# RWKV chunk recurrence: one run of state products and one run of value products in place of alternating ones

## The chip, the cores and the metric

The kernel runs on one core of a Trainium2 chip. Its time is the device time of one execution in microseconds (us), from the first to the last instruction of the core. Besides the timed runs there is one execution recorded by the hardware profiler; all rows below are of that execution. The engines are named as in the profile: PE is the tensor engine's matmuls, PEld its weight loads, DVE the vector engine, ACT the scalar engine, POOL the GpSimd engine, SP the engine that issues most DMAs.

## The reference

The kernel computes one transformer layer on 512 tokens of 1024 features in fp32: a norm, an input projection, two mixers side by side (sparse attention with three branches on one half of the features, an RWKV-7 recurrence with 8 heads of 64 on the other), an output projection, a second norm and a squared-ReLU feed-forward of width 4096. The change lies in the recurrence, which the reference states token by token:

```python
def step(state, inp):
    r_t, w_t, k_t, v_t, a_t, b_t = inp
    sa = jnp.einsum('bhvk,bhk->bhv', state, a_t)
    state = state * w_t[:, :, None, :] + sa[..., None] * b_t[:, :, None, :] + v_t[..., None] * k_t[:, :, None, :]
    return state, jnp.einsum('bhvk,bhk->bhv', state, r_t)
```

## The kernel before

**The recurrence by chunks.** The 512 tokens are 4 tiles of 128 (index `i`), and each tile is two chunks of 64 (index `c`); `q` counts the 8 chunks. Within a chunk all tokens are worked on at once, and only the state of 8 heads (64 by 64 each) goes from chunk to chunk. Heads lie in pairs: `e` is the half of the 128 partitions, rows 0 to 63 or 64 to 127, and `f` (0 to 3) counts the pairs. Each function of a tile's work is a Python generator, a *stream*: `rw_prep(i)` makes the decayed queries and keys (`AR`, `BK`) and the products `GA` and `YL`; `rw_inv(i)` inverts the triangular matrices (`QU`); `rw_vals(i)` makes the values (`UV`) and `LV`; `rw_chain(q)` is the serial step, and `rw_out(i)` norms its result.

**One step of the chain** (line 723) has three groups of products on PE, all through one PSUM bank (`pq_`, one buffer). `pp` (line 736) multiplies the state with the keys, 8 products; DVE adds it to `LV`. `puu` (line 743) multiplies by the inverse, 8 products; ACT and DVE copy it to `UV` (lines 744 and 745). `py` has two halves: `py[:, 1]` is the chunk's output, the state times the queries (line 752, left out at `q` = 0) plus the values' product (line 754); `py[:, 0]` is what is added to the state (line 755). Lines 760 and 761 on DVE make the new state `Sn`, and line 763 on ACT copies the output to `YY`. For each of the 8 pairs `(f, e)` line 752 is issued, then 754, then 755, and then the next pair. A product of line 752 has 64 rows and 64 columns of the array (64*64 in a profile row), one of lines 754 and 755 has 128 rows and 64 columns (128*64). Each fp32 product stands in the trace as two PE instructions, so `py` is 48 instructions in a chunk, or 32 at `q` = 0.

**What sets the order.** `merge` (line 129) runs the streams by a clock of its own: a stream yields the tensor-engine time that it assumes and a delay, or a condition on other streams, and the stream of the highest priority that is due goes on. On top of this the tile framework, which schedules by a simulated timeline, places each instruction in its engine's queue; each queue is then worked off in order. So between the chain's products stand products of the attention (`sc` line 1072, `pT` line 1108, `pv` lines 1121 to 1125), of the inverse (line 681) and of the input projection (`pa`, lines 332 to 334). After the chain of the last tile, `wo_load` (line 1146) loads and splits the output weights through two `wr` buffers into places that the chain's `ar`, `uv` and `yl` tiles leave, and `outproj` (line 1177) uses them. The feed-forward comes last, from line 1264 on.

Of the kernel before, what the change touches and what calls it, by code (L numbers as in the profile page):

```python
# [16 lines left out]
# T tokens in NT tiles, D features in KD tiles; the rest orders the streams of work and their loads  # L17
T = 512
# [40 lines left out]
# places in SBUF: size of each in bytes, and how many  # L59
# [8 lines left out]
# columns of the constant array  # L68
# [46 lines left out]
def layer(ctx: ExitStack, tc: tile.TileContext, A, cst, out):  # L115
# [7 lines left out]
    # ------------------------------------------------------------- scheduling  # L123
    # Work is written as streams: a stream yields (time on the tensor engine, delay until what it
    # waits for is there), or a condition on the other streams, and the streams are merged by that.
# [30 lines left out]
    # ------------------------------------------------------------------ pools  # L156
# [24 lines left out]
    def cycle(*places):  # L181
        """Allocation that goes round some places."""
        k = [0]

        def f(shape, name, dt=F32):
            k[0] += 1
            return at(places[(k[0] - 1) % len(places)], shape, name, dt)
        return f
# [4 lines left out]
    # -------------------------------------------------------------- constants  # L193
# [15 lines left out]
    def gain_load(src, place):  # L209
        """Gains per feature, in all partitions."""  # L210
        g_ = [at(place[b], [128, 512], "gain") for b in range(2)]
        for b in range(2):
            nc.sync.dma_start(g_[b], src[0:1, b * 512:(b + 1) * 512].partition_broadcast(128))
        return g_
# [33 lines left out]
    # vectors that are used per feature, 128 features to a row  # L248
# [49 lines left out]
    # ---------------------------------------------------------------- helpers  # L298
    def rsqrt(v, n, key, p=128):
        """1/sqrt of a small array of positive numbers."""  # L300
        y = small(n, "rs_y" + key)[0:p]
        G.tensor_tensor(y, v, bc(MH[0:p], [p, n]), op=ALU.pow)
        return y
# [3 lines left out]
    def split(raw, shape, hi=None, lo=None, eng=V):  # L307
        """A matrix in two parts, which add up to it exactly."""
        hi = (hi or w_hi)(shape, "whi", F32R)
        lo = (lo or w_lo)(shape, "wlo", F32R)  # L310
        S.copy(hi, raw)  # L311
        eng.tensor_tensor(lo, raw, hi.bitcast(F32), op=ALU.subtract)  # L312
        return hi, lo
# [22 lines left out]
    def norm_T(i, x_, gain, NH_, NL_, place, pool, raw=None):  # L336
        """Token tile i, normed, into the features' layout, in two parts."""
        ss = small(2, "ss")
        tmp = [at(place, [128, 512], "nt") for _ in range(2)]
        for b in range(2):  # L340
            S.activation(tmp[b], x_[b], AF.Square, scale=1.0 / 32, accum_out=ss[:, b:b + 1])
        vv = small(1, "vv")
        V.scalar_tensor_tensor(vv, ss[:, 0:1], 1e-6, ss[:, 1:2], op0=ALU.add, op1=ALU.add)
        rs = rsqrt(vv, 1, 'n')
        for b in range(2):
            V.scalar_tensor_tensor(tmp[b], x_[b], rs, gain[b], op0=ALU.mult, op1=ALU.mult)
            pt = pool([128, 4, 128], "pt")
            for kk in range(4):
                PE.transpose(pt[:, kk, :], tmp[b][:, kk * 128:(kk + 1) * 128], ident)
            S.copy(NH_[b][:, i], pt)  # L350
            if raw:
                S.copy(raw[b], pt)
            V.tensor_tensor(NL_[b][:, i], pt, NH_[b][:, i].bitcast(F32), op=ALU.subtract)

    # ------------------------------------------------------------ input norm
# [5 lines left out]
    def xk(k, i0=0, i1=NT):  # L361
        """The rows of a group of features, for tokens tiles i0 to i1."""
        return XH[k // 4][:, i0:i1, k % 4, :], XL[k // 4][:, i0:i1, k % 4, :]
# [6 lines left out]
    # =============================================================== RWKV  # L370
# [30 lines left out]
    # blocks of projected columns in the order of their use  # L401
# [6 lines left out]
    def turn_of(n):  # L408
        """A part of the input products waits for the one before it."""
        k = ORD.index(n)  # L410
        return lambda: ('in', ORD[k - 1]) in done if k else 'rw_kr' in done
# [8 lines left out]
    def raw_piece(p_):  # L420
        """A piece before it is split."""
# [6 lines left out]
    def piece(c0, h):  # L428
        """The next piece of the input weights; those after it are on their way."""
# [13 lines left out]
    def feat_cols(c0, use, halves=False):  # L443
        """Two tiles of 128 projected columns, features in the partitions."""
# [83 lines left out]
    def rw_prep(i):  # L528
# [49 lines left out]
        # products of keys with queries  # L578
# [26 lines left out]
    def rw_vals(i):  # L605
# [3 lines left out]
        # values, tokens in the partitions: odd heads in rows 0-63, even ones in rows 64-127  # L609
# [9 lines left out]
        # the bonus takes the place of the values in their other layout  # L619
# [25 lines left out]
    def rw_inv(i):  # L645
# [3 lines left out]
        # inverse of the triangular matrices: blocks of 32, merged from 2 up  # L649
# [73 lines left out]
    def rw_chain(q):  # L723
# [22 lines left out]
        yield 0.7, 0.8  # L746
        py = pq_([128, 2, 4, 64], "py")
        for f in range(4):
            for e in range(2):
                uv = UV[e][:, 4 * c + f, :]  # L750
                if q:
                    PE.matmul(py[ROW[1 - e], 1, f, :], AR[c][ROW[e], f, 1, :], S_[ROW[e], f, :],  # L752
                              start=True, stop=False)
                PE.matmul(py[ROW[1 - e], 1, f, :], YL[e][c][:, f, 1 - e, :], uv, start=not q, stop=True)  # L754
                PE.matmul(py[ROW[e], 0, f, :], YL[e][c][:, f, e, :], uv, start=True, stop=True)
# [8 lines left out]
        yield 1.8, 1.5  # L764
# [47 lines left out]
    # =============================================================== NSA  # L812
# [11 lines left out]
    def nsa_consts():  # L824
        # gains of the keys, with those of the queries and the scale
# [7 lines left out]
    def tok_cols(c0, n, use):  # L833
        """Projected columns, tokens in the partitions."""
# [12 lines left out]
    def compress(kind, ckv):  # L847
        """Compressed keys (0) or values (1)."""
# [66 lines left out]
    def keys(b, kb):  # L915
        """Keys of branch b: normed, in two parts, transposed."""
# [55 lines left out]
    def nsa_in():  # L972
# [4 lines left out]
        def cmp_in(j, pa):  # L977
            """Each token's features with those of the next one below them."""
# [11 lines left out]
        def kv_parts(b, i, pa, o0):  # L990
            """Columns o0 on of those of keys and values."""
# [49 lines left out]
    def attn_scores(i, g):  # L1041
# [5 lines left out]
        # compressed branch  # L1047
# [14 lines left out]
        # scores of the two other branches  # L1062
# [75 lines left out]
    # =============================================================== output  # L1138
# [53 lines left out]
    def norms():  # L1192
# [6 lines left out]
        for i in range(NT):  # L1199
# [6 lines left out]
            # differences of the normed tokens for the products by blocks  # L1206
# [20 lines left out]
    def run_more():  # L1227
        # the streams that others start
# [34 lines left out]
    # =============================================================== feed-forward  # L1263
# [12 lines left out]
    def blocks(b):  # L1276
        """The parts of a pair of tiles of features that its products by blocks take, in the order of their use."""
# [18 lines left out]
    def ahead_of(gens, n):  # L1296
        """What the generators give, made n parts ahead."""
# [46 lines left out]
    def pair_blocks(b):  # L1344
        """Products by blocks of two (Winograd's form of Strassen's): 7 for the 8."""
# [84 lines left out]
```

## Time and profile before

| | us |
|---|---|
| timed runs, median of 3 (lowest, highest) | 816.68 (814.18, 823.08) |
| profiled execution, first to last instruction | 818.9 |
| its PE busy time | 797.5 (97%) |
| its DVE, ACT, POOL busy time | 511.0, 395.9, 174.1 |
| from the start of the chain's first `py` (187.7) to the end of its last (410.5) | 222.8 |
| feed-forward and what follows the output projection's weights, from 440 on | 379 |

A busy PE in these rows is not a PE at its peak, since matmuls are pipelined and their ends are modelled; the distance from one instruction's start to the next one's start is what an instruction takes of the engine. The granted clock of PE stands in the rows as a share: 1.0 is 2.4 GHz and 0.5 is 1.2 GHz.

### The profile page before, as it was taken

Reading aid. Unit: us, or ns where it says so; the run is one execution under the profiler, and the core shown is the slowest. Engines: PE = TensorE matmul, PEld = TensorE weight load, DVE = VectorE, ACT = ScalarE, POOL = GpSimd, SP = SyncE. Lnnn points to the kernel's source line nnn. Section 1 sums busy time; section 2 is a strip of 40 time slices with the busy share of each in tenths; the row PEclk is TensorE's granted clock in tenths of the full one; section 3 lists DMA queues with packets and bytes.
Section 4 is the critical chain, followed back from the end, with each engine's and each line's share of the span. In section 5 each row is a group of like instructions: output and inputs, shape, how many; then the busy total and the mean of one; then the engine's idle time right before and its main releaser. Section 6 shows DMA issues by size and latency. Waiting matters only on the chain.

```text
span 818.9 us, 18281 instructions
## 1 busy us (share of the span) xinstructions
PE 797.5 (97%) x7357; PEld 684.4 (84%) x7357; DVE 511.0 (62%) x1157; ACT 395.9 (48%) x928; POOL 174.1 (21%) x176
## 2 busy tenths in 40 slices
PE   7999999999989999999999999999999999999998
PEld 5888888988878787887777889998888999978886
DVE  6344385674575399488764699986333799963333
ACT  6343334345353476569643564675332366663320
POOL 4002042312241252344320024310001323100000
PEclk9999999999975799599999999999999999999999
DMA  6741321120000000020134223314332343133212
GB/s 225 207 116 52 79 80 56 29 54 14 3 15 1 28 3 2 1 68 15 40 103 117 90 77 108 102 51 142 99 98 88 114 117 104 59 111 114 90 52 103
DMA packets 67338, 62.00 MB, mean 76 GB/s; under 512 B 6013, under 2 KB 53299, under 8 KB 67254
## 3 DMA queue, kind: packets, MB, share of 16 engines
q1 hardware_dynamic: 67254, 60.83, 24.9%
q8 instruction: 58, 0.95, 0.5%
q14 instruction: 26, 0.21, 0.1%
HBM read 58.72 MB, written 2.10 MB: 74 GB/s over the span
## 4 chain that ended last, share of the span: by engine, by line
PE 79%; DVE 11%; ACT 4%; DMA 3%; issue 2%; SPq 1%; POOL 0%; DVEq 0%; ACTq 0%; POOLq 0%
PE pa L332 7%; PE pa L333 7%; PE pa L334 7%; PE po L332 7%; PE po L333 7%; PE po L334 7%; PE pw L333 4%; PE pw L334 4%; PE pw L332 3%; PE sc L1072 3%; PE pg L586 2%; DVE wlo L312 2%; PE py L754 2%; PE py L752 2%; DMA wraw<-in_w_out_dram 2%
## 5 line engine op out<-in xcount | busy, mean ns | idle before, releaser
L311 ACT CAST whi<-wraw 128x512 fp32r<-128x512 f32 (+1 forms) x128 | 78.7, 622 | 141.5 <-PE po L333 29.1
L312 DVE TENSOR_TENSOR wlo<-wraw,whi 128x512 fp32r<-128x512 f32 (+1 forms) x120 | 86.2, 721 | 93.6 <-ACT whi L311 87.8
L332 PE MATMUL po<-whi 128*128 128x512 f32 x256 | 100.6, 394 | 1.6 <-DVE cc L1358 1.6
L333 PE MATMUL po<-wlo,whi 128*128 128x512 f32 x256 | 101.0, 395 | 0.0
L334 PE MATMUL po<-whi,wlo 128*128 128x512 f32 x256 | 100.7, 393 | 0.0
L333 PE MATMUL pw<-TT,whi 128*128 128x256 f32 x224 | 63.2, 282 | 0.0
L334 PE MATMUL pw<-TT,wlo 128*128 128x256 f32 x224 | 63.0, 281 | 0.0
L332 PE MATMUL pw<-TT,whi 128*128 128x256 f32 x224 | 62.5, 279 | 0.0
L332 PEld LDWEIGHTS po<-whi 128*128 128x128 f32 x256 | 48.0, 188 | 13.5 <-ACT whi L311 2.0
L334 PEld LDWEIGHTS po<-whi,wlo 128*128 128x128 f32 x256 | 48.1, 188 | 11.4
L333 PEld LDWEIGHTS po<-wlo,whi 128*128 128x128 f32 x256 | 48.1, 188 | 11.0
L332 PE MATMUL pa<-XH,whi 128*128 128x512 f32 (+1 forms) x144 | 53.6, 377 | 1.0 <-ACT XH L350 1.0
L333 PE MATMUL pa<-XL,whi 128*128 128x512 f32 (+1 forms) x144 | 54.4, 379 | 0.0
L334 PE MATMUL pa<-XH,wlo 128*128 128x512 f32 (+1 forms) x144 | 53.5, 374 | 0.0
L1086 POOL TENSOR_SCALAR P<-P,z 128x128 f32<-128x128 f32 (+3 forms) x32 | 35.6, 1122 | 77.9 <-DVE z L1035 35.5
L1288 POOL TENSOR_TENSOR ws<-wq 128x512 f32<-128x512 f32 x14 | 21.5, 1533 | 138.4 <-DMA wq<-in_w_ff_dram 123.4
L312 DVE TENSOR_TENSOR wlo<-ws,whi 128x512 fp32r<-128x512 f32 x56 | 48.1, 870 | 3.1 <-ACT whi L311 3.0
L311 ACT CAST whi<-ws 128x512 fp32r<-128x512 f32 x56 | 33.0, 618 | 34.8 <-PE pw L334 10.0
L312 DVE TENSOR_TENSOR wlo<-H,whi 128x512 fp32r<-128x512 f32 x32 | 22.1, 689 | 42.3 <-PE po L333 32.7
L334 PE MATMUL pw<-NH,wlo 128*128 128x256 f32 x168 | 47.0, 280 | 0.0
L333 PE MATMUL pw<-NL,whi 128*128 128x256 f32 x168 | 46.8, 279 | 0.0
L332 PE MATMUL pw<-NH,whi 128*128 128x256 f32 x168 | 46.8, 279 | 0.0
(319 smaller groups left out, 2109.8 us busy)
## 6 DMA issues: line engine op xcount, KB each, us to landing
wraw<-in_w_ff_dram SPq DMA_DIRECT2D x72, 256.0 KB
wq<-in_w_ff_dram SPq DMA_DIRECT2D x56, 256.0 KB
wraw<-in_w_in_dram SPq DMA_DIRECT2D x40, 256.0 KB
wraw<-in_w_in_dram SPq DMA_DIRECT2D x8, 268.0 KB
x<-in_x_dram SPq DMA_DIRECT2D x8, 256.0 KB
y<-in_x_dram SPq DMA_DIRECT2D x8, 256.0 KB
wraw<-in_w_out_dram SPq DMA_DIRECT2D x8, 256.0 KB
wraw<-in_w_out_dram SPq DMA_DIRECT2D x16, 128.0 KB
```

The source lines that it names most:

```text
L311: S.copy(hi, raw)
L312: eng.tensor_tensor(lo, raw, hi.bitcast(F32), op=ALU.subtract)
L332: PE.matmul(o_, l[0], r[0], start=first, stop=False)
L333: PE.matmul(o_, l[0], r[1], start=False, stop=False)
L334: PE.matmul(o_, l[1], r[0], start=False, stop=last)
L586: PE.matmul(pg[:, f], BK[ROW[e], 2 * f + c].rearrange("p a b -> p (a b)"), AR[c][ROW[e], f].rearrange("p a b -> p (a b)"), start=True, sto ...
L752: PE.matmul(py[ROW[1 - e], 1, f, :], AR[c][ROW[e], f, 1, :], S_[ROW[e], f, :], start=True, stop=False)
L754: PE.matmul(py[ROW[1 - e], 1, f, :], YL[e][c][:, f, 1 - e, :], uv, start=not q, stop=True)
L1072: PE.matmul(sc[:, h - h0, :], Qt[:, h, :], KT[br, g, hl].rearrange("p i t -> p (i t)")[:, 0:w], start=hl == 0, stop=hl == 1)
L1086: (G if (h, br) in SCG else V).tensor_scalar(P_[:, h, 0:w], P_[:, h, 0:w], z[:, h:h + 1], None, op0=ALU.mult)
L1288: G.tensor_tensor(s3, q[0][0], q[1][0], op=ALU.subtract)
```

## The change

In a chunk, all 8 products of the state with the queries (line 752) are issued first, and then the 16 products of the values (now line 757), in the same order of pairs. Only the first product in each half of the partitions opens the bank (`start`), where before every product with the queries and every one of line 755 did. The time that the stream tells `merge` for the group goes from 1.8 to 1.6. Comments are taken out elsewhere, and the lines after 755 move by 3.

```diff
         py = pq_([128, 2, 4, 64], "py")
-        for f in range(4):
-            for e in range(2):
-                uv = UV[e][:, 4 * c + f, :]
-                if q:
-                    PE.matmul(py[ROW[1 - e], 1, f, :], AR[c][ROW[e], f, 1, :], S_[ROW[e], f, :],
-                              start=True, stop=False)
-                PE.matmul(py[ROW[1 - e], 1, f, :], YL[e][c][:, f, 1 - e, :], uv, start=not q, stop=True)
-                PE.matmul(py[ROW[e], 0, f, :], YL[e][c][:, f, e, :], uv, start=True, stop=True)
+        FE = [(f, e) for f in range(4) for e in range(2)]
+        if q:
+            for f, e in FE:
+                PE.matmul(py[ROW[1 - e], 1, f, :], AR[c][ROW[e], f, 1, :], S_[ROW[e], f, :],
+                          start=f == 0, stop=False, skip_group_check=True)
+        for f, e in FE:
+            uv = UV[e][:, 4 * c + f, :]
+            for a, r in ((1 - e, 1), (e, 0)):
+                PE.matmul(py[ROW[a], r, f, :], YL[e][c][:, f, a, :], uv,
+                          start=not q and f == 0 and e == 0, stop=True, skip_group_check=True)
...
-        yield 1.8, 1.5
+        yield 1.6, 1.5
```

The last step (`q` = 7) shows the plain case. On PE its `py` stood so before (the first two pairs and the last):

```order
L1108 MATMUL pT<-identr,P 128x128 x8
L752 MATMUL py<-Sn,AR 64x64
L754 MATMUL py<-UV_2928,YL_2774 64x64
L755 MATMUL py<-UV_2928,YL_2774 64x64
L752 MATMUL py<-Sn,AR 64x64
L754 MATMUL py<-UV_2929,YL_2776 64x64
L755 MATMUL py<-UV_2929,YL_2776 64x64
...
L752 MATMUL py<-Sn,AR 64x64
L754 MATMUL py<-UV_2929,YL_2776 64x64
L755 MATMUL py<-UV_2929,YL_2776 64x64
L1121 MATMUL pv<-th,VH 128x512
```

and stands so now (`pv` at line 1124 is the one at 1121 before):

```order
L1111 MATMUL pT<-identr,P 128x128 x8
L752 MATMUL py<-Sn,AR 64x64 x8
L757 MATMUL py<-UV_2928,YL_2774 64x64 x2
L757 MATMUL py<-UV_2929,YL_2776 64x64 x2
...
L757 MATMUL py<-UV_2929,YL_2776 64x64 x2
L1124 MATMUL pv<-th,VH 128x512
```

The 24 products stand between the same neighbours; the 8 of line 752 are now together ahead of the 16. In the step `q` = 3 other work stands inside the group, and the scheduler moved it. A piece of the difference on PE there (`pd` and `pz` are of the inverse, `pbn` of the values of the next tile):

```order
-L752 MATMUL py<-Sn,AR 64x64
-L754 MATMUL py<-UV_1831,YL_1599 64x64
-L681 MATMUL pz<-Tn,qm 32x32 x29
+L757 MATMUL py<-UV_1831,YL_1599 64x64
+L757 MATMUL py<-UV_1830,YL_1597 64x64 x2
+L757 MATMUL py<-UV_1831,YL_1599 64x64 x2
+L681 MATMUL pz<-Tn,qm 32x32 x30
 L534 MATMUL pu<-W2A,THA 128x512
-L681 MATMUL pz<-Tn,qm 32x32 x3
-L755 MATMUL py<-UV_1831,YL_1599 64x64
```

Here the last products of `py` now come ahead of `pz` and `pu` (of the next tile's preparation), where one of them came behind both.

On SP, the piece of the queue that reloads `x` for the output projection (`y`) and loads the output weights, as a difference:

```order
-L1181 DMA y_5749<-in_x_dram 128x512
-L1156 DMA wraw<-in_w_out_dram 128x512 x4
-L1181 DMA y_5777<-in_x_dram 128x512
-L1161 DMA wraw<-in_w_out_dram 64x512 x4
+L1184 DMA y_5749<-in_x_dram 128x512
+L1159 DMA wraw<-in_w_out_dram 128x512 x4
+L1164 DMA wraw<-in_w_out_dram 64x512 x2
+L1184 DMA y_5777<-in_x_dram 128x512
+L1164 DMA wraw<-in_w_out_dram 64x512 x2
```

Two half-size loads of the output weights now stand ahead of the second reload, where all four stood behind it. The other moves on PE, DVE and ACT are of single instructions past a few neighbours in the attention from `q` = 3 on.

## Rows read from the trace of the kernel before

**Rows 1.** The page: busy time by engine, and the granted clock in 40 slices.

```profile
PE 797.5 (97%) x7357; PEld 684.4 (84%) x7357; DVE 511.0 (62%) x1157; ACT 395.9 (48%) x928; POOL 174.1 (21%) x176
PEclk9999999999975799599999999999999999999999
```

**Rows 2.** Busy time by stretch: PE, PEld, DVE, ACT, POOL, granted clock, DMA share, GB/s.

```profile
200.00:233.40 33.40, 30.86 (x699) 26.54 (x698) 20.41 (x41) 13.38 (x31) 12.30 (x12) 1.00 0.01 3
233.40:274.40 41.00, 40.24 (x284) 34.98 (x284) 21.77 (x99) 18.15 (x70) 8.83 (x9) 0.50 0.02 7
274.40:329.00 54.60, 53.30 (x966) 41.75 (x962) 45.31 (x147) 36.27 (x104) 19.92 (x19) 1.00 0.04 12
329.00:346.10 17.10, 17.10 (x116) 14.51 (x116) 7.14 (x43) 8.51 (x35) 6.02 (x8) 0.50 0.00 1
440.00:819.00 379.00, 371.17 (x2241) 328.04 (x2239) 238.55 (x396) 169.51 (x324) 50.01 (x36) 1.00 0.31 95
```

**Rows 3.** Timeline of PE, py at q = 1: start, length, instruction.

```profile
200.62 0.33 PE L752 MATMUL py<-Sn,AR 64*64 64x64 f32 x2
200.88 0.27 PE L754 MATMUL py<-UV,YL 128*64 128x64 f32 x1
...
201.14 0.33 PE L752 MATMUL py<-Sn,AR 64*64 64x64 f32 x2
...
204.78 0.75 PE L681 MATMUL pd<-Z,Q 32*32 32x32 f32 x64
```

**Rows 4.** Timeline of PE, py at q = 2, first row and the row behind.

```profile
251.73 0.47 PE L752 MATMUL py<-Sn,AR 64*64 64x64 f32 x2
...
258.23 2.08 PE L1072 MATMUL sc<-KT,QT 128*128 128x256 f32 x8
```

**Rows 5.** Timeline of PE, py at q = 0, first row and the row behind.

```profile
187.72 0.27 PE L754 MATMUL py<-UV,YL 128*64 128x64 f32 x1
...
188.80 1.16 PE L586 MATMUL pg<-AR,BK 64*128 64x128 f32 x8
```

**Rows 6.** Chain of waits, pp at full and at half clock: start, us.

```profile
192.52 0.61 PE pp L736 x16
265.18 1.05 PE pp L736 x16
```

**Rows 7.** Instructions of py alone, by stretch (q = 3 to 7): columns as in rows 2.

```profile
279.10:287.00 7.90, 4.59 (x48) 3.33 (x48) 0.00 (x0) 0.00 (x0) 1.00 0.10 33
326.10:332.50 6.40, 5.39 (x48) 3.85 (x48) 0.00 (x0) 0.00 (x0) 0.73 0.00 0
351.40:355.60 4.20, 4.20 (x48) 3.08 (x48) 0.00 (x0) 0.00 (x0) 1.00 0.00 2
394.30:398.50 4.20, 4.19 (x48) 3.08 (x48) 0.00 (x0) 0.00 (x0) 1.00 0.01 2
406.30:410.50 4.20, 4.18 (x48) 3.09 (x48) 0.00 (x0) 0.00 (x0) 1.00 0.31 106
```

**Rows 8.** Who PE waited for, 180 to 480 us: total, times, longest.

```profile
PE pz L702 <- DVE Tn L694: 3.6, 2, 3.1
```

**Rows 9.** Chain of waits, where it runs through DVE after q = 1 and q = 3.

```profile
223.85 0.35 DVE kkn L561
...
234.16 1.07 PE pz L702 x32
...
296.50 0.56 DVE P L1076
...
312.15 0.93 DVE wlo L312
```

**Rows 10.** Timeline of DVE around q = 5 (in brackets idle time before, and what ended it).

```profile
355.40 0.74 DVE L312 TENSOR_TENSOR wlo<-wraw,whi 128x512 fp32r<-128x512 f32 x1 [1.38 <-PE py L752]
...
357.36 0.41 DVE L760 TENSOR_TENSOR Sn<-py,Sn 128x256 f32<-128x256 f32 x1
```

**Rows 11.** Timeline behind q = 7: ACT and SP.

```profile
410.08 1.14 ACT L311 CAST whi<-wraw 128x512 fp32r<-128x512 f32 x2 [2.84 <-PE py L755]
...
412.62 1.11 SPq L1161 DMA_DIRECT2D wraw<-in_w_out_dram  x2
```

**Rows 12.** Chain of waits behind it: a load of output weights on the path.

```profile
419.91 3.92 DMA wraw<-in_w_out_dram
```

## The prediction

> **What bounds the kernel now.** Read the page first: PE is busy for 797.5 of 818.9 us [rows 1], so the engine that the change touches is the one that is nearly always occupied. Its granted clock, though, is not full all the way: in the 40 slices there are fives and sevens a third of the way in. The table by stretch shows where: 1.0 from 200 to 233.4, 0.50 (1.2 GHz) from 233.4 to 274.4, 1.0 again to 329.0, and 0.50 to 346.1 [rows 2]. PE is busy for nearly the whole of each of these stretches. The feed-forward from 440 on, 379 us, has no step of the chain in it and stays as it is.
>
> Then the timeline of PE, which tells what the group `py` costs. Read distances between starts, not lengths. At q = 1 the pair of line 752 starts at 200.62 and the next one at 201.14, so a pair (f, e) takes 0.52 us; eight of them take 204.78 - 200.62 = 4.16 us [rows 3]. Inside a pair, the first instruction of line 754 starts 0.26 after that of line 752, and the next pair 0.26 after that. At half clock the same 48 instructions take 258.23 - 251.73 = 6.50 us [rows 4].
>
> Two other rows show the same shapes without alternation. At q = 0 there is no line 752, and the 32 instructions of the values take 188.80 - 187.72 = 1.08 us [rows 5], where in the alternating group they have 8 x 0.26 = 2.1. `pp`, 16 instructions of the shape of line 752 (64*64), takes 0.61 us at full clock and 1.05 at half [rows 6], where line 752 now has 2.1. So the alternating group takes 4.16 us for what costs 0.61 + 1.08 = 1.69 us when each kind stands by itself. Something is paid at each passage between the two kinds, some 0.15 us (4.16 - 1.69 = 2.47, spread over 16 passages of which one remains).
>
> Last, the waits and the chain of waits, for whether PE's time is the kernel's time. PE waits little: the largest sum is 3.6 us, for DVE's `Tn`, nearly all in one wait of 3.1 us [rows 8]. But the chain leaves PE three times: through DVE from 223.85 to 234.16 and from 296.50 to about 313 [rows 9], and at the end through ACT, DVE and the loads of the output weights [rows 11, 12].
>
> **The change, part by part.** It removes no product and adds none: 24 a chunk as before, 16 at q = 0. What it removes is the alternation.
>
> - q = 1, 6 and 7, full clock, nothing between [rows 3, 7]: 4.16 becomes 1.69; 2.47 each, 7.4 together.
> - q = 5, full clock too [rows 7], but DVE decides here: before it starts `Sn` at 357.36 it has other work, and its only idle time in that place is 1.38 us, ended by `py` [rows 10]. The state cannot come sooner by more than about that, while PE's next products do come sooner by 2.47. Bounds 1.4 and 2.5; I take 2.0, between them, because the work that follows on PE here is of the attention and does not need the state.
> - q = 3, full clock, with the inverse and the next tile's work inside: its own rows fill 4.59 us [rows 7]. The new order keeps two pieces inside, so two more passages at 0.15: 1.69 + 0.3 = 2.0. Gain 2.6; take 2.5.
> - q = 2, all at half clock: 6.50 now. After: 1.05 for line 752 [rows 6], and for the values between 1.08 x 6.50/4.16 = 1.7 and, at twice their time at full clock, 2.2. Gain 3.3 to 3.8; take 3.5.
> - q = 4: its own rows fill 5.39 us, and the clock falls at 329.0 inside it [rows 2, 7]. If the new group runs at full clock the gain is 5.39 - 1.69 = 3.7; if wholly at half, 5.39 - 2.95 = 2.4. Take 3.0.
>
> PE's sum is 7.4 + 2.0 + 2.5 + 3.5 + 3.0 = 18.4 us. What of it reaches the end? In the stretches where the chain runs on PE, all. The two stretches through DVE begin with a product of PE (`kkn` at 223.85 waits for one, `P` at 296.50 for a score), so their start moves with PE; what they can keep is what DVE could not have started sooner. From 274.4 to 329.0 DVE is busy 45.3 of 54.6 us [rows 2], the fullest stretch of the chain; I let it keep 0.5. The stretch behind q = 7 begins with ACT's cast of an output weight, which sat idle for 2.84 us until `py` was done, because it writes into a tile that `py` reads [rows 11]; the loads follow one another from there, 3.92 us for one [rows 12], so this end moves with `py` too. The two weight loads that moved up in SP's queue pass one reload, whose data is not used until the output projection; I cost that at nothing, covered by those same waits, and at one load's 0.5 us of issue (1.11 for two) if it is not.
>
> The smaller edits: fewer opening products change no count and no shape, so nothing. The yield of 1.6 for 1.8 moves the planner's clock, not the chip's, and the moves of single instructions from q = 3 on have no row; I bound them by the largest waits that PE has for one line in this region other than the 3.1, about 0.5 us (3.6 - 3.1) either way.
>
> Sum: 18.4 - 0.5 = about 18 us. The profiled execution has 818.9, 2.2 above the median of the timed runs, 816.7. 818.9 - 18 = 800.9, and against the median 816.7 - 18 = 798.7: **799 us**.
>
> A rule of the Trainium skill speaks against part of this. The row first: 32 value instructions in 1.08 us are 34 ns each, weight load included [rows 5]. The page "TensorE: Matmul & The Clock Gate", section "Part 3: Packing small matmuls — row/col tiling", says that a weight load overlaps running matmuls only where the row groups differ, and the section "LDWEIGHTS (loading the stationary operand)" prices it at the columns over 1.2 per ns. The values use all rows, so an estimate from that page is 32 x 64/1.2 = 1.7 us for them and a gain of 1.8 instead of 2.47 a chunk, about 5 us less in all. The row at q = 0 disagrees, and it is the very same instructions, so the sum goes by the row.
>
> **The rivals.**
>
> 1. *The clock gains too.* It fell at 329.0, inside the slow group of q = 4, and stayed low for 17.1 us [rows 2]; behind the group of q = 2 it was low as well. If the shorter group leaves PE better filled and that fall does not come, what stands at half clock behind the group, from about 332.5 to 346.1, 13.6 us, takes 13.6 x 0.61/1.05 = 7.9 [rows 6]: 5.7 less, and 0.7 at q = 4. 799 - 6 = **793**. For it: the place of the fall. Against: the groups of q = 1, 5 and 6 ran at full clock throughout, so the group alone does not do it.
> 2. *Part of the gain stays with DVE.* If the stretch at 296.5 and the one at q = 5 do not move with PE, the gains of q = 1, 2, 3 and 5 are eaten there in part; half of 2.5 + 3.5 + 2.5 + 2.0 is 5, with the whole of the 3.5 at worst 9. **806**. For it: DVE is at 83% there. Against: it was idle and waiting for a product at the head of that stretch.
> 3. *The values stay at the alternating rate.* If their pace is not that of q = 0 when they add to what line 752 wrote, they keep 2.1 us and the group takes 2.7; 7 x 1.0 less gain, **806**. Only the adding speaks for it; the products of the input projection add into a bank at their usual pace. The rule on weight loads of the page "TensorE: Matmul & The Clock Gate" would act in this direction.
> 4. *A longer wait puts PE at half clock: slower.* The 3.1 us wait before line 702 [rows 8] ends just after the clock has fallen at 233.4, and 41 us at half follow [rows 2]. If PE, ahead by 8 us after q = 3, runs into a wait of that length between 296 and 313, the rest of that stretch, 33 us of work to 329, goes at half: 33 x (1.05/0.61 - 1) = 24 more. 799 + 24 = **823**. It decides from a single wait of some 3 us; now PE's waits there are far below that, and the order there hardly changed. The page "TensorE: Matmul & The Clock Gate", section "HAM oscillation — how this bites in real kernels", tells of such a return to half rate after each wait for data; the fall at 233.4 agrees.
> 5. *It does not do what it says*: the passages cost nothing and the group is slow for another reason. No change, **817**. The three rows of `py`, `pp` and q = 0 leave little room.
>
> **How the numbers follow.** Forecast 0.52; rivals 1 to 5: 0.26, 0.10, 0.04, 0.05, 0.03. The forecast's own spread is the bounds above, 2 to 3 us, and as much for the spread of the runs (814.2 to 823.1 now): 795 to 803. The range reaches to the low side of rival 1 and over most of 2 and 3: **788 to 807**; outside lie rivals 4 and 5, a third of 2 and 3, and a little of 1, together under 0.2. A change under 1%, about 8 us, can hardly be told from none here. Faster by over that, below 808.5: 0.52 + 0.26 + 0.09 + 0.03 = 0.90, less a little for error in the base: 0.89. Slower by over 1%, above 825: 0.02, the half of rival 4 that is longer, and 0.01 for the unforeseen: 0.03. Within: 0.08.
>
> **What would show it.** In the profile after, at q = 1 the distance from the first row of line 752 to the row behind the last of line 757 should be 1.7 us, with 0.6 for line 752 and 1.1 for line 757; at half clock, where that still occurs, about 3. PE's busy time should fall by about 18 us while DVE's stays near 511. The chain's length from the first `py` to the end of the last should fall from 222.8 to about 205, and what follows the last `py` should keep its length. If `py` is short and the chain is not, rivals 2 or 4 hold, told apart by the granted clock. If line 757 takes 2 us, it is rival 3. I am wrong altogether if the distance between rows of line 752 does not drop when they stand together.

## The result, and the profile after

Over four runs each, the changed kernel takes 785.7 us (783.8 to 786.3), the kernel before 817.9 (814.2 to 823.1): a ratio of 0.960, 95% interval 0.955 to 0.965. The forecast was 799, so the sum gave 18 us and the chip 32. The two profiled executions lie further apart than the medians: 818.9 and 781.9 us of span, 37 us. One execution, the traced one of the kernel with half the passages (below), took 1449 us and stands in no median.

The page of the kernel after has the same two rows as [rows 1]: busy time by engine, and the granted clock in 40 slices.

```profile
PE 759.8 (97%) x7357; PEld 657.5 (84%) x7357; DVE 511.8 (65%) x1157; ACT 395.6 (51%) x928; POOL 175.2 (22%) x176
PEclk9999999999985999999999999999999999999999
```

PE has the same 7357 instructions and 37.7 us less busy time, DVE has what it had. And the row of the clock has one dip where [rows 1] has two. By stretch (columns as in [rows 2]):

```profile
198.20:230.20 32.00, 28.69 (x729) 25.39 (x728) 22.01 (x46) 12.96 (x31) 11.80 (x12) 1.00 0.04 11
230.20:250.70 20.50, 20.50 (x164) 19.00 (x164) 12.56 (x65) 10.71 (x48) 5.37 (x5) 0.50 0.01 2
250.70:296.00 45.30, 43.62 (x875) 35.50 (x875) 39.04 (x129) 31.33 (x92) 20.04 (x20) 1.00 0.04 14
296.00:325.00 29.00, 29.00 (x490) 24.39 (x490) 25.29 (x105) 25.04 (x83) 10.82 (x11) 1.00 0.01 2
404.00:782.00 378.00, 370.80 (x2239) 327.72 (x2237) 238.60 (x396) 169.29 (x324) 50.27 (x36) 1.00 0.31 95
```

Before, PE stood at half clock (1.2 GHz) for 41.0 us behind 233.4, for 17.1 behind 329.0 [rows 2], and for 3.4 behind 410.9 (too short to show as a dip in [rows 1]): 61.4 us.

```profile
410.90:414.30 3.40, 3.40 (x13) 2.68 (x13) 2.80 (x4) 0.59 (x2) 1.15 (x1) 0.50 0.10 27
```

Now it does so once, for 20.5 us. The feed-forward, the last row, is as it was. The group itself, on the timeline of PE after, at q = 1 and at q = 2:

```profile
198.22 0.68 PE L752 MATMUL py<-Sn,AR 64*64 64x64 f32 x16
198.83 1.15 PE L757 MATMUL py<-UV,YL 128*64 128x64 f32 x32
199.91 0.75 PE L681 MATMUL pd<-Z,Q 32*32 32x32 f32 x64
...
246.24 1.12 PE L752 MATMUL py<-Sn,AR 64*64 64x64 f32 x16
247.29 1.97 PE L757 MATMUL py<-UV,YL 128*64 128x64 f32 x32
249.19 0.58 PE L1075 MATMUL sc<-KT,QT 128*128 128x256 f32 x1
```

Between starts, the group of q = 1 takes 199.91 - 198.22 = 1.69 us (4.16 in [rows 3]): 0.61 for line 752 and 1.08 for the values, to the hundredth what `pp` and q = 0 had shown [rows 5, 6]. At half clock it takes 249.19 - 246.24 = 2.95 (6.50 in [rows 4]). The longest wait of PE [rows 8] is still there:

```profile
PE pz L702 <- DVE Tn L694: 3.1, 1, 3.1
```

**Where the 37 us are.** The same step of the chain can be looked up in both traces, and the lead of the new kernel read off at each. It starts 2.4 us ahead at the first `py` (187.72 [rows 5], now 185.31), because in that execution the clock rose sooner at the start of the program (products of 256 columns of the input projection take 0.21 us from start to start there until 18.4, and in the new trace 0.12 from 14.6 on); the kernel before does so too in other executions (186.76 in the second trace of it, below). Then (a row that names a step alone goes on to the first `py` of the next step; q = 2 ends with its own `py`, q = 3 with `pp` of q = 4, and q = 7 with ACT's cast behind it):

| stretch | lead gained, us | of it group | of it clock |
|---|---|---|---|
| q = 1, to `pp` of q = 2 | 2.5 | 2.5 | |
| to the first `py` of q = 2 | 0.6 | | 0.6 |
| q = 2 itself | 3.5 | 3.5 | |
| to the first `py` of q = 3 | 6.4 | | 6.4 |
| q = 3 | 3.2 | 3.2 | |
| DVE's stretch, to `py` of q = 4 | -1.0 | -1.0 | |
| q = 4 | 9.9 | 3.3 | 6.6 |
| q = 5 | 2.4 | 2.4 | |
| q = 6 | 2.0 | 2.0 | |
| q = 7 | 2.1 | 2.1 | |
| on to the feed-forward | 2.3 | | 1.4 |
| the feed-forward | 0.6 | | |

Groups 18.0, clock 15.0, and 3.9 of the start and the end that neither explains. The row of q = 4 is split by the rows of `py` alone, which filled 5.39 us there [rows 7], partly at half clock, and now (first row, the second is q = 3, 4.59 before):

```profile
308.40:311.20 2.80, 2.09 (x48) 1.75 (x48) 0.00 (x0) 0.00 (x0) 1.00 0.00 0
263.70:267.30 3.60, 2.26 (x48) 1.88 (x48) 0.00 (x0) 0.00 (x0) 1.00 0.21 70
```

5.39 - 2.09 = 3.3 are the group's, and the rest is put down to the clock: the 13.6 us at half clock behind the group alone are worth 13.6 x (1 - 0.61/1.05) = 5.7 [rows 6]. In the row behind q = 7, 1.4 is what 3.4 us at half clock cost: 3.4 x (1 - 0.61/1.05) [rows 6].

### The profile page after: what moved, and what is told of

It reads as the page before. It is cut to its first block, busy times and chain, and to the rows that moved or that the text cites. A ratio compares the mean times of both kernels' runs of the same rounds, so it can differ in the third digit from the quotient of the medians.

```text
span 781.9 us, 18278 instructions
## 1 busy us (share of the span) xinstructions
PE 759.8 (97%) x7357; PEld 657.5 (84%) x7357; DVE 511.8 (65%) x1157; ACT 395.6 (51%) x928; POOL 175.2 (22%) x176
## 4 chain that ended last, share of the span: by engine, by line
PE 84%; DVE 7%; ACT 4%; DMA 3%; issue 1%; SPq 1%; POOL 0%; DVEq 0%; ACTq 0%; POOLq 0%
PE pa L332 8%; PE pa L333 8%; PE pa L334 8%; PE po L332 7%; PE po L333 7%; PE po L334 7%; PE pw L333 5%; PE pw L334 5%; PE pw L332 5%; PE pg L586 2%; PE sc L1075 2%; DMA wraw<-in_w_out_dram 1%; PE py L757 1%; PE pT L1111 1%; PE pz L681 1%
```

## The experiments

In short: the first theory is that the passages between two kinds of instruction cost time by themselves and that the alternating groups bring and hold the half clock; the rivals are that the clock's stretches lie elsewhere by chance, that the opening products count, or that any thin work does it. All times are against the kernel before on the same chip (818 to 819 us there), with rounds of their own, and letters in a quoted expectation hold for that one. In the six kernels that put the alternation back in some groups, the new body is this; only the condition differs:

```diff
+        if COND:
+            for f, e in FE:
+                uv = UV[e][:, 4 * c + f, :]
+                PE.matmul(py[ROW[1 - e], 1, f, :], AR[c][ROW[e], f, 1, :], S_[ROW[e], f, :], ...)
+                PE.matmul(py[ROW[1 - e], 1, f, :], YL[e][c][:, f, 1 - e, :], uv, start=False, ...)
+                PE.matmul(py[ROW[e], 0, f, :], YL[e][c][:, f, e, :], uv, ...)
+        else:
             ...
```

**All groups alternate, with the new opening products.**

```diff
+        if q:          # start= f == 0 for the state's products, the first pair only for the others
```

> The changed kernel with the alternation put back in all chunks, but with the new opening products (one in each half of the bank, and one more for the first value product, which has no state product before it there). Theory (the alternation is all that costs): the time of the kernel before, 818 us (814 to 823), groups of 4.16 us at full clock, half clock for some 60 us. Rival (the many opening products cost something): clearly under 818, groups shorter than 4.16 us; if they were the whole of it, 786 us.

821.2 us; ratio 1.003 (1.001 to 1.006). The whole gain is gone, with the new opening and the yield of 1.6 kept, so the gain comes from the order of the products, and the two smaller edits are worth nothing that can be seen. Its half-clock stretches (by stretch, columns as above):

```profile
201.90:208.70 6.80, 6.80 (x104) 5.84 (x102) 3.71 (x9) 0.77 (x2) 0.73 (x1) 0.50 0.01 2
236.00:266.70 30.70, 30.70 (x206) 26.88 (x205) 17.09 (x86) 14.02 (x59) 5.36 (x5) 0.50 0.01 1
328.20:341.80 13.60, 13.60 (x92) 11.83 (x94) 6.72 (x40) 7.54 (x33) 3.65 (x6) 0.50 0.01 1
393.00:399.80 6.80, 6.80 (x35) 5.03 (x35) 4.06 (x9) 2.34 (x5) 0.64 (x1) 0.50 0.12 33
```

58 us at half clock: the first, third and fourth begin inside or right behind the alternating groups of q = 1, 4 and 6, with PE busy throughout.

**The groups one by one.**

```diff
+        if q == 2:
```

> The changed kernel (785.7 us, half clock for about 20 us from 230 to 251) with the alternation put back at q = 2 alone. Theory A (the slow group keeps the clock low): the group takes 6.5 us in place of 2.95, and the half-clock stretch lasts some 35 to 41 us as before the change, 3.5 + 6.4 = 10 us more, about 795.5. Theory B (the group costs its own length, the clock depends on when the work around it comes): 3.5 us more, about 789, the stretch some 24 us, longer by the group alone.

```diff
+        if q == 4:
```

> The changed kernel with the alternation put back at q = 4 alone. Theory A (the slow group brings the fall of the clock): the clock falls in or behind that group for some 17 us, 2.5 to 3.6 + 5.4 us more, about 794. Theory B (the fall before came from the moment): no fall there, 2.5 us more, about 788.

```diff
+        if q in (1, 5, 6, 7):
```

> The changed kernel with the alternation put back at q = 1, 5, 6 and 7, where the clock was full before and after. Both theories: 4 x 2.47 = 9.9 us more, about 795.6, and the half-clock stretch of some 20 us as it was; theory A allows a short fall behind q = 7 (3.4 us before) for 1 to 2 us more. If much less than 9.9 comes back, other engines set the time there.

```diff
+        if q == 3:
```

> The changed kernel (785.7 us) with the alternation put back in the group of q = 3 alone. The groups put back at q = 2 (794.2), q = 4 (798.0) and q = 1, 5, 6, 7 (798.3) cost 8.5, 12.3 and 12.6 us, 33.4 together; all seven cost 35.5 (821.2). Theory A, that the parts add: q = 3 costs what is left, 2.1, which is also its own passages, 2.5 less what the inverse's pieces inside it cost anyway; 788 us, group 4 to 4.6 us at full clock. Rival, that this group too can bring a fall of the clock when it stands alone: 3 to 9 us more, 792 to 797, with a half-clock stretch beginning in or right behind the group.

| alternating at | us | ratio to before | cost over 785.7 |
|---|---|---|---|
| q = 2 | 794.2 | 0.972 (0.968 to 0.976) | 8.5 |
| q = 4 | 798.0 | 0.975 (0.972 to 0.978) | 12.3 |
| q = 3 | 788.7 | 0.964 (0.960 to 0.967) | 3.0 |
| q = 1, 5, 6, 7 | 798.3 | 0.976 (0.973 to 0.979) | 12.6 |
| sum | | | 36.4 |
| all | 821.2 | 1.003 (1.001 to 1.006) | 35.5 |

The parts add up, within some 3 us on each cost by the intervals of the ratios; the 3.0 of q = 3 alone are not clear of that. They are what its passages cost, and its group (5.7 us, but for two instructions that stand behind other work) ran at full clock. For q = 2 the group is worth 3.55 and the cost is 8.5; the stretch around it lasts 30.7 us where it was 20.5 (theory A had 35 to 41, theory B 24):

```profile
229.60:260.30 30.70, 30.70 (x221) 27.05 (x219) 16.94 (x82) 12.86 (x55) 5.36 (x5) 0.50 0.02 7
```

For q = 4 the group is worth some 3.3 and the cost is 12.3, 4 us over theory A. Why is in its trace: the timeline of PE in the group (lines 753, 755 and 756 are the former 752, 754 and 755), and the stretches around it.

```profile
315.39 0.33 PE L755 MATMUL py<-UV,YL 128*64 128x64 f32 x2
315.65 0.98 PE L597 MATMUL ptb<-identr,BK 64*128 64x64 f32 x8
316.56 0.47 PE L756 MATMUL py<-UV,YL 128*64 128x64 f32 x2
316.97 0.47 PE L753 MATMUL py<-Sn,AR 64*64 64x64 f32 x2
```

```profile
308.00:315.90 7.90, 7.90 (x72) 6.14 (x70) 7.17 (x27) 5.62 (x18) 4.29 (x4) 1.00 0.01 2
315.90:332.90 17.00, 17.00 (x124) 14.43 (x126) 6.73 (x40) 8.51 (x36) 4.98 (x7) 0.50 0.00 1
332.90:340.00 7.10, 7.10 (x208) 6.30 (x208) 4.88 (x16) 5.79 (x16) 0.88 (x2) 1.00 0.02 3
```

The group began at 312.0; at 315.9 the clock falls inside it, and a pair of instructions of one kind, up to the next start, goes from 0.26 to 0.41 us. In the kernel after, the same place (308.5 to 311.1) is at full clock and so is all that follows (the row 296.00:325.00 above). The alternation of this one group brings the fall: over 14 traces (all but that of the kernel with half the passages), a fall comes in or right behind the group of q = 4 in all five where it alternates, and in none of the nine where it does not. The 17 us at half clock are its main price, worth 7 us by [rows 6]. For q = 1, 5, 6 and 7 no fall came in a group of the traced execution; of the 12.6, four groups at 2.5 are 10. That trace also has 6.8 us more at half clock than the kernel after (23.9 in the first stretch, and 3.4 from 455.4 on, behind a wait of 1.42 us), which are worth 2.9; what brought them is not shown.

**Whole-array products ahead of the group.** Does PE lose its clock in this place because it is held up, and does dense work bring it back? Twenty-four products of the identity (128 rows, 128 columns), later overwritten:

```diff
+        if q == 4:
+            for _ in range(24):
+                PE.matmul(py[:, 0, 0:2, :]..., identr, identr, start=True, stop=True, ...)
```

> The changed kernel with 24 extra products of the identity with itself (128 rows, 128 columns, written to the bank of the group and overwritten) ahead of the group at q = 4: PE is held up there by some 2.4 us, as long as the alternation held it up, but at full work. Theory A (the clock falls because the alternating group does little work for 4 us): no fall, about 788. Rival (any hold-up of that length at this place shifts the work behind and brings the fall): a fall of some 17 us as with the alternation at q = 4 alone (798.0), so 795 to 798.

```diff
+        if q == 2:     # the same 24 products
```

> The same 24 extra products ahead of the group at q = 2, inside the half-clock stretch: some 3.6 us at half clock. Theory A (what ends the half clock is dense work): the stretch ends no later than 251, at best 3 us sooner, and the time is 785 to 789. Rival (the stretch lasts for a set amount of work behind the wait): it is longer by the extra products, as with the alternation at q = 2 (30.7 us, 794.2).

795.4 us (ratio 0.972, 0.970 to 0.975) and 807.5 (0.988, 0.985 to 0.991). At q = 4 the products take 2.81 us, and no fall comes in the group or for 22 us after it (first row), as theory A had it. But other instructions moved with them, and falls of 3.4 and 6.8 us come later, behind waits of 1.05 and 2.34 us of PE, so the total says little. At q = 2, where the clock was already low, they bring nothing back, against theory A: 27.3 us at half clock, 5.3 of them these products (second row, of the second kernel), and later waits of 1.9 and 3.9 us with falls of 3.4 and 10.2.

```profile
315.85:335.40 19.55, 19.55 (x533) 17.16 (x531) 14.74 (x53) 13.69 (x47) 6.86 (x10) 1.00 0.10 30
```

```profile
233.00:260.30 27.30, 27.30 (x194) 25.34 (x193) 14.54 (x71) 10.93 (x48) 6.86 (x7) 0.50 0.01 2
```

**Thin work of one kind in the place of the passages.**

```diff
+        if q == 4:
+            for _ in range(9):
+                for f, e in FE:
+                    PE.matmul(py[ROW[1 - e], 1, f, :], AR[c][ROW[e], f, 1, :], S_[ROW[e], f, :], start=True, stop=True, ...)
```

> The changed kernel with the eight state products of q = 4 issued ten times in a row in place of once (the nine first are overwritten): some 2.75 us more of 64*64 products at one array mode, ahead of the same group. It fills the time that the alternating group took (4.4 us in all) without its passages. The alternating group of this chunk brought a fall of the clock at once (the experiment with q = 4 alone: half clock from 315.9 for 17.0 us, group begun at 312.0); the same time filled with whole-array identity products brought none within 20 us. Theory A1, the passages between modes bring it: no fall in or within 4 us behind the group; 786 + 2.8 = 788 to 796, the upper end from the instructions that move behind it. Theory A2, little work of the array in a time brings it, whatever the reason: a fall inside or right behind the group and 10 to 17 us at half clock, 794 to 800.

803.6 us (ratio 0.980, 0.975 to 0.985), above what either theory gave. The total is spoilt again by what moved behind the group: the values of q = 4 now stand behind other products, a wait of 2.1 us appears, and a fall of 6.8 us with it at 343.7. The place it was made for is clear, though:

```profile
312.46:318.48 6.02, 6.02 (x164) 5.68 (x163) 3.64 (x19) 3.45 (x14) 4.06 (x4) 1.00 0.01 3
318.48:341.90 23.42, 21.06 (x647) 17.95 (x644) 13.11 (x43) 13.24 (x40) 6.13 (x8) 1.00 0.16 48
```

Six us of 64*64 products but for a few, longer than it took from the start of the alternating group of q = 4 to any of its five falls (2.9 to 5.2 us), and the clock stays at 1.00 there and for 23 us behind, as theory A1 had it. So in this place a run of thin products does not bring the fall; their alternation with the other kind does. This is one trace.

**Half the passages.** State products of one feature pair, then its four values, and so on: 8 runs, 7 passages inside a group in place of 15.

```diff
-        for f, e in FE:
+        for f in range(4):
+            for e in range(2):
+                PE.matmul(py[ROW[1 - e], 1, f, :], AR[c][ROW[e], f, 1, :], S_[ROW[e], f, :], ...)
+            for e in range(2):
+                ...
```

> The changed kernel with a coarser alternation: for each of the four f two products of line 752 and then four of the values, in all chunks; 7 passages in a group where the changed kernel has 1 and the kernel before 15. Theory (each passage costs some 0.15 to 0.18 us, whatever is opened): a group of 1.69 + 6 x 0.165 = 2.7 us at full clock, 7 us for the seven groups, about 793 without a fall at q = 4 and 799 with one. Rival (the cost lies in changing the half of the array from product to product): the group stays near 1.7 us, 786.

794.9 us (ratio 0.973, 0.970 to 0.976): 9.2 over the kernel after, where all passages cost 35.5. Seven groups with six passages more, at 0.15 to 0.18 each (2.47 us over 16 or 14 of them), would be 6.5 to 7.5 of it. The trace does not bear out that price. PE keeps there, from start to end, the pace that the other traces show at half clock: 1.04 us for `pp` (1.05 in [rows 6]) and 1.93 for the values at q = 0, although its mean granted clock stands as 1.000. In order, the values of q = 0, `pp` of q = 1 and `py` of q = 1, with the row behind each (lines 753 and 758 are 752 and 757):

```profile
340.68 2.00 PE L758 MATMUL py<-UV,YL 128*64 128x64 f32 x32
342.61 0.65 PE L586 MATMUL pg<-AR,BK 64*128 64x128 f32 x2
...
349.19 1.11 PE L736 MATMUL pp<-Sn,AR 64*64 64x64 f32 x16
350.23 0.27 PE L597 MATMUL ptb<-identr,BK 64*128 64x64 f32 x1
...
362.66 0.34 PE L753 MATMUL py<-Sn,AR 64*64 64x64 f32 x4
362.93 0.66 PE L758 MATMUL py<-UV,YL 128*64 128x64 f32 x8
363.52 0.33 PE L753 MATMUL py<-Sn,AR 64*64 64x64 f32 x4
...
366.06 0.52 PE L681 MATMUL pd<-Z,Q 32*32 32x32 f32 x28
```

The group takes 366.06 - 362.66 = 3.40 us, 0.43 more than 1.04 + 1.93, so six passages more cost 0.07 each; in the group that alternates throughout, 14 passages more cost 6.50 - 2.95 = 3.55 at half clock, 0.25 each. By that one trace the price of a passage depends on how long the runs between are, and is no constant. Seven groups at 0.43 make 3.0 us at that pace; what the other 6 of the 9.2 are, and what this group takes at full clock, is open.

**The wait of 3.1 us.** What would fill or shorten it? Seven float32 products of 256 columns in the inverse of tile 1 (overwritten), and, in another kernel, DVE's four bonus products ahead of `Tn` (2.05 us) put on POOL:

```diff
+            if i == 1 and l == 4:
+                for _ in range(7):
+                    PE.matmul(pd, Zt[:, 0:4, :]..., Zt, start=True, stop=True, ...)
```

> The changed kernel with 7 extra fp32 products of 256 columns (some 3 us) in the bank of pd, at the last stage of the inverse of tile 1, where PE then waits 3.1 us for DVE; their result is overwritten, nothing is left out. Theory (that wait is what brings the clock down at 230 us): no half clock from 230 to 251, the extra products stand in the wait, 8 us less, about 778. Rival (the weak work behind the wait, scores on few columns and products of 64 rows, brings it down by itself): the clock falls all the same some us later, 784 to 789.

```diff
-        for f in range(4):
-            V.scalar_tensor_tensor(rkp[:, f, :], ZR[:, f, :], vec('rk', f), ZK[:, f, :], ...)
+        if i == 1:
+            G.tensor_tensor(rkp, ZR, bc(vec('rk', 0, 4)..., [128, 4, 128]), op=ALU.mult)
+            G.tensor_tensor(rkp, rkp, ZK, op=ALU.mult)
+        else: ...
```

> The changed kernel with the four products of the bonus (line 622, 2.05 us on VectorE) of token tile 1 put on GpSimd as two, so that VectorE comes to Tn 2 us sooner and the 3.1 us wait of the tensor engine before line 702 shrinks to about 1. Some other instructions move with it. Theory A, the wait alone brings the fall at 230 us: the 20.5 us at half clock go or come in one short piece; 2 us of wait and 5 to 10 us of clock less, 774 to 780. Rival B, the narrow work behind the wait (32*32 products of the inverse, 64-row products of keys with queries, 32-column scores) brings it as well: the wait shrinks, a stretch of 15 to 25 us at half clock stays, 783 to 787.

805.5 us (ratio 0.984, 0.981 to 0.988) and 798.7 (0.974, 0.969 to 0.979): both slower than the kernel after, and both outside what either theory gave. In both, the wait before line 702 is gone, and the clock falls all the same (a row by stretch of the one, then of the other):

```profile
236.00:259.90 23.90, 23.90 (x281) 21.16 (x283) 14.94 (x63) 13.52 (x52) 7.80 (x7) 0.50 0.01 2
```

```profile
233.70:254.20 20.50, 20.50 (x158) 18.67 (x156) 14.20 (x76) 12.63 (x54) 6.04 (x5) 0.50 0.00 1
```

In the second, a wait of 1.6 us for DVE's `YR` stands in its place; in the first, one of 0.75 us, over 4 us ahead of the fall, and short runs of 32*32, 64-row and 32-column products between. Both have new waits later, with falls behind them. That the wait of 3.1 us alone brings the long stretch is not shown; that taking it away in these two ways does not help is.

**The kernel before again, and all groups but one.**

```diff
+        if q and q != 2:
```

> The kernel before once more, unchanged, for a second trace of it. In its first trace the tensor engine stood at half clock from 233.4 for 41.0 us; the changed kernel with all seven groups alternating stood there for 30.7, and the changed kernel and the experiments with the group of q = 2 as changed stood there for 20.5 or 23.9. Theory A, the alternating group of q = 2 keeps the half clock on by 7 us or more: again 27 us or more behind the wait, and a second stretch from about the group of q = 4. Rival, the length is chance from run to run and the group has no part in it: 20 to 24 us can come in this kernel too.

> The changed kernel with the alternation put back in all groups but that of q = 2, against the one with all seven (821.2 us). Theory A, the group of q = 2 by itself costs its passages at half clock (3.55 us) and lengthens the stretch at half clock that the wait before it began: 821.2 - 8.5 = 812.7, between 811 and 815, with 20.5 to 24 us at half clock from about 235, and the falls at q = 1, 4 and 7 as with all seven. Rival, only its passages count and the length is chance: 817 to 818, and the stretch as likely 27 to 41 us.

The kernel before took 816.0 us in this one execution; all groups but q = 2 take 810.4 (ratio 0.990, 0.987 to 0.994), 10.8 less than with all seven and a little under the range. The stretches of the kernel before, second trace (without one of 3.4 us at 473.8, beside a wait of 1.42 us), then of all groups but q = 2:

```profile
204.10:207.50 3.40, 3.40 (x75) 3.00 (x61) 2.72 (x8) 0.37 (x1) 0.73 (x1) 0.50 0.02 5
234.80:265.60 30.80, 30.80 (x222) 27.03 (x222) 17.09 (x84) 12.97 (x55) 5.37 (x5) 0.50 0.02 8
327.00:340.70 13.70, 13.70 (x86) 11.66 (x89) 6.52 (x37) 8.18 (x35) 3.86 (x6) 0.50 0.01 1
350.90:354.30 3.40, 3.40 (x74) 2.76 (x73) 2.40 (x4) 1.69 (x6) 1.50 (x2) 0.50 0.38 125
```

```profile
232.90:256.80 23.90, 22.66 (x198) 20.87 (x198) 15.35 (x75) 10.88 (x48) 5.38 (x5) 0.50 0.04 13
321.70:335.30 13.60, 13.60 (x92) 11.83 (x94) 6.74 (x40) 7.57 (x33) 3.69 (x6) 0.50 0.01 1
386.50:393.30 6.80, 6.80 (x37) 5.02 (x35) 4.05 (x9) 2.29 (x5) 0.97 (x1) 0.50 0.13 35
```

With q = 2 alternating, the first long stretch lasted 41.0, 30.7, 30.7 and 30.7 us in four traces; with q = 2 as changed, and nothing added to it, 20.5 or 23.9 in all seven. Of the difference 3.55 is the group's own; 3 to 17 more are clock that comes back later. So the alternating group of q = 2 holds the half clock on, as theory A has it in both expectations; the 41.0 of the first trace were the long end of that. The falls at q = 4 come again in both kernels. Those at q = 1 and q = 5 come in the first alone, one at q = 6 in the second alone, and none at q = 7, so not all where they were expected.

## Why the prediction was off

The price of the alternating group as a whole was right (that a single passage has a fixed price was not shown, by the kernel with half the passages); the term that failed is the clock, which the sum took over from the trace of before as it stood.

1. **q = 1, 6 and 7, 2.47 each: right for the groups** (4.16 to 1.69 at each). On the path 2.5 at q = 1, and a little less at q = 6 (2.0) and q = 7 (2.1).
2. **q = 5, 2.0 between bounds of 1.4 and 2.5: right, a little low.** 2.4. DVE's `Sn` starts 3.23 us behind the first `py` (323.82) where it was 5.96 [rows 7, 10]:

```profile
325.65 0.41 DVE L694 TENSOR_TENSOR Tn<-Tn,pd 128x256 f32<-128x256 f32 x1
...
327.05 0.41 DVE L763 TENSOR_TENSOR Sn<-py,Sn 128x256 f32<-128x256 f32 x1
```

3. **q = 3, 2.5: low.** 3.2 on the path.
4. **q = 2, 3.5: right for the group** (6.50 to 2.95, 3.55). The sum put the clock behind it at nothing, and 6.4 us of sooner full clock stand right behind it.
5. **q = 4, 3.0: right for the group**, 3.3, since it now runs at full clock; and 6.6 us of clock come with it.
6. **0.5 kept by DVE: 1.0.** The stretch moved with PE nearly whole, as argued.
7. **The end moves with the last `py`: right.** ACT's cast starts at 376.05, once `py` is done, after 0.51 us of idle time in place of 2.84 [rows 11]:

```profile
376.05 1.14 ACT L311 CAST whi<-wraw 128x512 fp32r<-128x512 f32 x2 [0.51 <-PE py L757]
```

From there to the end of the span it is 405.9 us, 408.8 before (818.9 - 410.1 [rows 11]); 1.4 of the difference is the third fall, which is gone. The two loads that moved up cost nothing that can be seen.

The groups together came to 18.0 us, which is what the sum had. **The step that failed** is that the sum gave the clock nothing, and left it to the first rival, which it also made too small. The clock was given a chance of 0.26 and 6 us; it was the case, and 15 us. Two readings were wrong in it. That "the groups of q = 1, 5 and 6 ran at full clock throughout, so the group alone does not do it" took one trace for a rule: over the seven traces in which alternating groups began at full clock, 11 of 30 such groups brought a fall (all five at q = 4, none of five at q = 3, the others now and then), and of the 24 grouped ones in the kernel after and in the four experiments that alternate at q = 2, at q = 3, at q = 4 and at q = 1, 5, 6 and 7, none. And only the fall at q = 4 was priced; that a group inside a stretch at half clock could hold it there was not thought of, though the first stretch, 41 us, held one.

What each microsecond costs was in the rows all the time: work that takes 1.05 us at half clock takes 0.61 at full [rows 6], so 40.9 us less at half clock are worth 40.9 x 0.42 = 17 us, of which the groups inside them had been counted in part.

Rival 4, a longer wait that puts PE at half clock, did not come: between 296 and 325 PE has no wait at all and the clock is 1.00. But it is no fancy: the fillers and the POOL edit, which made new waits of 1 to 4 us, each came with falls of 3.4 to 10 us behind them. The rival asked for one wait of some 3 us; falls came behind waits from 1.05 us on. Rival 3, with the rule on weight loads, is out: the values that add to what line 752 wrote take the 1.08 us of q = 0.

What stays open is what a passage consists of, why a group brings the fall in one execution and not in the next, and what starts the stretch at 230 us, which outlived both attempts on the wait before it.

## To carry to other kernels

Where small products of two shapes alternate on TensorE, issue each shape in one run: a group whose kind changed with every product or two took 4.16 us at full clock where two runs took 1.69, and the difference does not show as idle time. Before a sum is made over stretches at half clock, ask of each what began it and what work in it could hold it; a shorter stretch at half clock can be worth as much as the work that was cut. And a fill or a moved instruction that makes new waits on TensorE can cost more than it saves: the five kernels with such an edit here came out 10 to 22 us over the kernel after.

## What the hardware did that was not expected

- The clock fell to half while PE was, by every record, busy. Of 41 stretches at half clock between 100 and 700 us in 14 traces, 28 begin beside a wait of PE (the shortest 1.05 us, most 1.4 to 3.9), 2 with only shorter ones near (0.75 and 0.96), and 11 with none, in or right behind an alternating group. The section "HAM oscillation — how this bites in real kernels" of the page "TensorE: Matmul & The Clock Gate" of the Trainium skill tells of a fall at each wait for data, of some 3 to 5 us there; the 28 agree with it in kind, but 14 of their waits are shorter, 1.05 to 2.64 us. Its section "A second HAM failure mode: psum-queue depth-cycling" tells of a kernel with many very short idle times between groups in which the clock went up and down. The 11 would be of that sort if PE idles in a passage; no record shows that.
- In a passage the cost is in the time to the next start, not in the length of a record: records of the alternating group overlap, and PE counts as busy for all 4.16 us [rows 3].
- The same code stands at half clock for different lengths: the first stretch of the kernels with q = 2 grouped for 20.5 or 23.9 us, that of the kernel before for 30.7 or 41.0. Between 100 and 700 us the two traces of the kernel before stand at half clock for 61.4 and 54.6 us, which is worth 2.9 of the 5.0 us between their spans (818.9 and 813.9).
